# Modulation dot products moved from the branch tiles to the last values and the attention; the scale of two feature tiles by dot products on VectorE

## Chip, cores and metric

One core of one Trainium2 chip. The metric is the time of one execution on the device in microseconds. The kernel before takes 1518.03 us, the median of 3 runs (1517.66 to 1518.57).

## The reference

One layer of a diffusion transformer over 256 latent and 256 context tokens, model width 2048, all in float32. The conditioning vectors `c` and `c_ctx` give six modulation vectors by one large product; the latent tokens go through a mixer of two attentions with gates, then through a convolutional feed-forward part:

```python
mod = silu(c) @ w_mod + b_mod;  mod_c = silu(c_ctx) @ w_mod + b_mod
sh1, sc1, gt1, sh2, sc2, gt2 = split(mod, 6)
h  = modulate(rms_norm(x,   g_attn_pre), sh1,  sc1)      # y * (1 + scale) + shift
hc = modulate(rms_norm(ctx, g_attn_pre), csh1, csc1)
qa, ka, va, qb, kb, vb, ga, gb = split(h @ w_in);  ka_c, va_c, kb_c, vb_c from hc @ w_in
oa = window attention (8 heads, 2 key heads, rotary, sinks);  ob = neighbourhood attention (8 heads)
y  = (sigmoid(ga) * (oa @ w_br_a) + sigmoid(gb) * (ob @ w_br_b)) @ w_o
x  = x + gt1 * rms_norm(y, g_attn_post)
x  = x + gt2 * rms_norm(conv_ffn(modulate(rms_norm(x, g_ffn_pre), sh2, sc2)), g_ffn_post)
```

## The kernel before

Every float32 product is done as three matmuls: each operand is split into a high part (ScalarE, a copy with rounding, L127) and a low part (VectorE, source minus high, L131), and TensorE adds high·high, high·low and low·high. Weights come as blocks of 1 MB through the SP queue into a ring of four buffers `raw` and are split into `wh` and `wl`, in halves (`halves`, L136). `block(ahead)` gives the next block, splits the one after it and issues loads further ahead. The order on each engine is fixed when the kernel is built: by hand for TensorE in the two key sweeps, elsewhere by a scheduler that keeps what the tiles need of each other; `issue_after(x)` puts an instruction behind x.

The stages, by the trace: a first key sweep to about 97 us, a second key sweep to 153, the values to 263, the attention with the queries and three gates (`fill`) to 428, the gate stage (gates `pg` and branches `pb`) to 682, the output projection to 769, the up projection to 1268, the down projection to 1508.

**First key sweep.** Six key heads (NK1) over 16 feature tiles k, three matmuls `pk` per head and tile (`keys`). The modulation scale of tile k+1 comes from narrow matmuls `pm` (`narrow`, L313: the silu vectors as 32 columns against a 1 MB unit of `wm_sc`), is evacuated by ScalarE (`evacuated`), transposed by small matmuls `ptm` and becomes `Gc` on VectorE (`scale_of`, L334), and from this the scaled features `h` (L352 high, L354 low). From k=3 on two tiles are done at a time. The key weights of tile k are split into `ku`. Squares of the features go into `ssq` (`squares`); a matmul `pss` with ones (L514), in k=13 after the fourth head, sums them over partitions, and `rs` is the reciprocal root. The shift of four feature tiles (ND) comes from dot products on VectorE: `load_sd(t)` loads 1 MB of rows into the one buffer `sd`, and `dot` (L427) multiplies it with the silu vector of the latents (v=0) or of the context (v=1); `load_sd(t+1)` follows the second. The first two of these dots stand in k=12 and k=14, six in the second sweep.

**Modulation dots.** `mods` (L204) multiplies a 1 MB unit of `wm_b` from the ring with the broadcast silu vector `crb` on VectorE, one unit per dot; one unit is held ahead (`load_mod`). There are 48 of them up to the output projection. In the values, `beside(1)` puts 20 key bias dots and then mods next to the steps kk of each weight block; the last values block (nb == 9) has none. The attention has none. In the gate stage each gate has one, except gates (1,1) and (2,0), and branch tiles j = 4, 6, 8, 9, 10, 11, 13 have one, so that such a tile has three.

**Attention.** Period p does `scores` of head p on TensorE (`s`), a half `fill`, `transposes` of the head before (`pt`, split into `h`), the other half `fill`, and `values` of the head before (`po`, L792). In between, VectorE does the softmax, the split of the next weights, of the next keys (`keys_of`) and of the values (`vals_of`, the last two set `last`).

The lines that hold the places of the dots:

```python
if nb and kk < (0 if nb == 9 else 2 if nb == 8 else 3 if nb % 2 else 4):
    beside(1)
...
mods(1 if (j, i) not in ((1, 1), (2, 0)) else 0, crb[:])          # in gate(j, i)
...
mods(1 if j in (4, 6, 8, 9, 10, 11, 13) else 0, crb[:])           # in branch tile j
```

Of the kernel before, what the change touches and what calls it, by code (L numbers as in the profile page):

```python
# [58 lines left out]
def layer_kernel(ctx, tc, xc, xt, ccol, crow, wm_sc, wm_sd, wm_sh, wm_b, cols, wk, wkt, ws, rope, mask_a, bias_b, out):  # L59
# [181 lines left out]
    with ExitStack() as mx:  # L241
# [10 lines left out]
        with ExitStack() as at:  # L252
# [4 lines left out]
            def rope_of(t, which, nm):  # L257
# [58 lines left out]
            def evacuated(k, n, pm):  # L318
                ev = up.tile([P, 2 * P], F32, tag="half", bufs=2, name=f"ev{k}")
                with ExitStack() as es:  # L320
                    if k == KT - 2:
                        es.enter_context(tc.issue_after(done_u[k][0]))
                    e_ = nc.scalar.activation(ev[:, : n * P], pm[:, : n * P], AF.Copy)
# [126 lines left out]
            for k in range(KT):  # L450
# [861 lines left out]
```

## Time and profile before

| what | value |
|---|---|
| median of 3 runs | 1518.03 us |
| the profiled execution | 1517.4 us |
| its span from first to last instruction | 1515.6 us |
| mean granted clock of TensorE | 0.998 of full speed |
| TensorE busy | 1501.2 us, 99% |
| VectorE busy | 1132.8 us, 75% |
| ScalarE busy | 780.6 us, 52% |
| moved by DMA | 382.13 MB, 252 GB/s in the mean |

A row of the timeline reads: start, duration, engine, line, operation, output tile <- input tiles, shapes, count; in brackets the idle time of the engine before it and what released it. Durations of neighbouring rows overlap by some hundredths to 0.16 us, because instructions are pipelined; the distance of two starts is what one costs. A row of windows reads: stretch, its length, busy time of each engine with its instructions, granted clock, share of the DMA engines' time, GB/s. A row of groups reads: line, engine, operation, tiles, shapes, count, busy us and mean ns of one, then the idle time before.

### The profile page before, as it was taken

How to read it: one execution, taken by the hardware profiler on the slowest of the kernel's cores; microseconds unless marked ns; L12 is line 12 of the kernel's file. 1: busy time of each engine (PE TensorE's matmuls, PEld its weight loads, DVE VectorE, ACT ScalarE, POOL GpSimd, SP SyncE). 2: the span in 40 equal slices, each digit the busy share in tenths (PEclk: the TensorE clock that was granted, in tenths of full speed). 3: DMA queues.
4: the chain of work that ended last, by engine and by line, in shares of the span. 5: the costliest groups of instructions: out<-in, count | busy, mean ns of one | idle time of the engine just before them, and what ended most of it. 6: DMA issues, size and time to landing. Idle time of an engine off the chain costs nothing.

```text
span 1515.6 us, 21653 instructions
## 1 busy us (share of the span) xinstructions
PE 1501.2 (99%) x8549; PEld 1288.8 (85%) x8549; DVE 1132.8 (75%) x1679; ACT 780.6 (52%) x1277; POOL 1.7 (0%) x10
## 2 busy tenths in 40 slices
PE   9999999999999999999999999999999999999997
PEld 7876889899888888888888888888888888888886
DVE  4496996888888989887778888888788776444444
ACT  4442443777765544454466555555555555344342
POOL 0000000000000000000000000000000000000000
PEclk9999999999999999999999999999999999999999
DMA  9988678433378989888956666666666556555552
GB/s 369 398 321 336 270 295 331 160 133 112 122 258 299 348 327 344 330 332 345 378 192 223 250 232 220 244 248 227 245 240 234 195 193 251 221 194 195 194 194 84
DMA packets 59255, 382.13 MB, mean 252 GB/s; under 512 B 6545, under 2 KB 6929, under 8 KB 16913
## 3 DMA queue, kind: packets, MB, share of 16 engines
q1 hardware_dynamic: 58432, 379.68, 67.1%
q8 instruction: 67, 1.10, 0.3%
q10 hardware_dynamic: 720, 1.07, 0.2%
q14 instruction: 36, 0.29, 0.0%
HBM read 376.48 MB, written 4.24 MB: 251 GB/s over the span
## 4 chain that ended last, share of the span: by engine, by line
PE 95%; DVE 3%; ACT 1%; issue 0%; DMA 0%; DVEq 0%; SPq 0%
PE pu L174 21%; PE py_d L880 16%; PE pu L175 11%; PE pk L439 7%; PE pv L654 7%; PE pg L174 6%; PE py_o L880 5%; PE pq L174 4%; PE pb L174 3%; PE pg L175 3%; PE pq L175 2%; PE pb L175 2%; PE po L792 1%; PE s L762 1%; PE pm L313 1%; DVE wl L131 1%
## 5 line engine op out<-in xcount | busy, mean ns | idle before, releaser
L131 DVE TENSOR_TENSOR wl<-raw,wh 128x1024 fp32r<-128x1024 f32 x444 | 528.6, 1221 | 224.7 <-ACT wh L127 224.3
L127 ACT ACTIVATE wh<-raw 128x1024 fp32r<-128x1024 f32 x444 | 451.3, 1053 | 276.4 <-PE py_d L880 129.1
L174 PE MATMUL pu<-h,wh 128*128 128x512 f32 x1404 | 488.0, 391 | 0.0
L175 PE MATMUL pu<-h,wl 128*128 128x256 f32 x1404 | 395.9, 282 | 0.0
L174 PEld LDWEIGHTS pu<-h,wh 128*128 128x128 f32 x1404 | 263.6, 188 | 55.6 <-issue 0.4
L175 PEld LDWEIGHTS pu<-h,wl 128*128 128x128 f32 x1404 | 265.4, 189 | 0.0
L880 PE MATMUL py_d<-wh,ff 128*128 128x512 f32 x704 | 216.6, 389 | 0.0
L174 PE MATMUL pg<-h,wh 128*128 128x512 f32 x464 | 161.8, 390 | 0.0
L880 PEld LDWEIGHTS py_d<-wh,ff 128*128 128x128 f32 x704 | 132.1, 188 | 27.3
L204 DVE SCALAR_TENSOR_TENSOR raw<-raw,crb 128x2048 f32<-128x2048 f32 x64 | 146.2, 2286 | 7.3 <-DMA raw<-in_wm_b_dram 5.4
L880 PE MATMUL py_d<-wl,ff 128*128 128x512 f32 x352 | 136.9, 389 | 0.0
L175 PE MATMUL pg<-h,wl 128*128 128x256 f32 x464 | 131.4, 283 | 1.5 <-DVE wl L131 1.5
L439 PE MATMUL pk<-h,ku 128*128 128x512 f32 x480 | 118.0, 398 | 0.7 <-DVE ku L131 0.4
L179 ACT ACTIVATE half_u<-pu 128x256 f32<-128x256 f32 x88 | 33.5, 383 | 152.3 <-PE pu L175 152.3
L439 PEld LDWEIGHTS pk<-h,ku 128*128 128x128 f32 x480 | 87.4, 188 | 25.3 <-issue 4.8
L174 PE MATMUL pq<-h,wh 128*128 128x512 f32 x304 | 108.5, 395 | 0.0
L174 PEld LDWEIGHTS pg<-h,wh 128*128 128x128 f32 x464 | 87.1, 188 | 18.0
L654 PE MATMUL pv<-wh,h 128*128 128x512 f32 (+1 forms) x384 | 101.7, 354 | 0.0
L174 PE MATMUL pb<-h,wh 128*128 128x512 f32 x256 | 90.2, 392 | 0.9 <-ACT wh L127 0.9
L175 PEld LDWEIGHTS pg<-h,wl 128*128 128x128 f32 x464 | 87.7, 189 | 3.0 <-DVE wl L131 2.9
L175 PE MATMUL pq<-h,wl 128*128 128x256 f32 x304 | 85.5, 281 | 0.0
L180 DVE TENSOR_TENSOR u<-pu,half_u 128x256 f32<-128x256 f32 x88 | 37.2, 423 | 56.7 <-ACT half_u L179 56.6
(193 smaller groups left out, 1787.1 us busy)
## 6 DMA issues: line engine op xcount, KB each, us to landing
raw<-in_ws_dram SPq DMA_DIRECT2D x222, 1024.0 KB, 4.8
raw<-in_wm_b_dram SPq DMA_DIRECT2D x64, 1024.0 KB, 4.9
raw<-in_wm_sc_dram SPq DMA_DIRECT2D x15, 1024.0 KB, 7.7
raw<-in_wm_sh_dram SPq DMA_DIRECT2D x16, 768.0 KB, 6.3
raw<-in_wkt_dram SPq DMA_DIRECT2D x10, 1024.0 KB, 5.0
crb<-sild SPq DMA_DIRECT2D x6, 1024.0 KB, 7.2
raw<-in_wk_dram SPq DMA_DIRECT2D x7, 768.0 KB, 8.2
sd<-in_wm_sd_dram SPq DMA_DIRECT2D x4, 1024.0 KB, 7.5
```

The lines of the kernel that those rows point to most:

```text
L127: a_ = nc.scalar.activation(hi, src, AF.Copy)
L131: v_ = nc.vector.tensor_tensor(out=lo, in0=src, in1=hi, op=ALU.subtract)
L174: nc.tensor.matmul(pt[:, :], wh[:, w], a, start=first and i == 0, stop=False, skip_group_check=True)
L175: nc.tensor.matmul(pt[:, :S], wl[:, w], a[:, 0], start=False, stop=last and i == n - 1, skip_group_check=True)
L179: a_ = nc.scalar.activation(t[:], pt[:, S:], AF.Copy)
L180: v_ = nc.vector.tensor_tensor(out=out_, in0=pt[:, :S], in1=t[:], op=ALU.add)
L204: nc.vector.scalar_tensor_tensor(out=r, in0=r, scalar=1.0, in1=row, op0=ALU.mult, op1=ALU.mult, accum_out=modx[:, j : j + 1])
L313: nc.tensor.matmul(pm[32 * j : 32 * j + 32, t * P : t * P + P], cc[:, q, :], rsc[k + t][:, q * P : q * P + P], start=q < 4, stop=q >= KT - ...
L439: nc.tensor.matmul(pk[:], wt[:, w], hh[:, :, k, a], start=k == 0 and a == 0 and wt is wh, stop=k == KT - 1 and a == 1)
L654: nc.tensor.matmul(pv[i][:, :nw], src[:, k, a, t0 : t0 + P], wt[:, w], start=k == 0 and q == 0, stop=k == KT - 1 and q == 2)
L762: nc.tensor.matmul(s_ps[:], qs[hd][:, a, qt * P : qt * P + P], k_, start=q == 0, stop=q == 2)
L880: p_ = nc.tensor.matmul(py[t][:], act[:, k, a, t * P : t * P + P], wt[:, w], start=k == 0 and q == 0, stop=k == nk - 1 and q == 2)
```

## The change

It does three things.

1. The scale of the feature tiles 14 and 15 (NC = 2) is no longer done by narrow matmuls. Their rows of the modulation weights go ahead of the ND tiles in `wm_sd`, so that there are six tiles t for `dot`; t = 0 and 1 give the scales. `load_sd(0)` is issued in k=9 instead of k=10; dots stand in k=10 and k=11 (one each), k=12 (two), k=14 (one) and seven instead of six in the second sweep. `scale_of(14, 2)` reads the sums from `sd0`, in k=13 at the second head.
2. Seven mods of the branch tiles are moved: three to the last values block, four to the attention periods 1, 4, 7 and 10 (behind `last[1]`), and the gates (1,1) and (2,0) get the two that the numbering then leaves.
3. To hold one row of silu values `crb` from the values to the gates, tiles are placed otherwise: the rotary tables in two tiles, the masks in five rows of `bz` instead of seven (loaded alternately), and the second load of `crb` falls away.

```diff
+NC = 2
...
-            sh0 = sp.tile([P, ND, 2], F32, name="sh0")
+            sd0 = sp.tile([P, NC + ND, 2], F32, name="sd0")
...
             def load_sc(k):
-                if k < KT:
+                if k < KT - NC:
                     rsc[k] = raw_block(wm_sc[k], parts=1 if k else 2)
...
-            def scale_of(k, n, ev):
-
-                pt = bank(f"ptm{k}")
-                for t in range(n):
-                    nc.tensor.matmul(pt[:, 2 * t : 2 * t + 2], ev[:, t * P : t * P + P], sel[:], start=True, stop=True)
+            def scale_of(k, n, ev=None):
+
+                if ev is None:
+                    pt = sd0[:].rearrange("p a b -> p (a b)")
+                else:
+                    pt = bank(f"ptm{k}")
+                    for t in range(n):
+                        nc.tensor.matmul(pt[:, 2 * t : 2 * t + 2], ev[:, t * P : t * P + P], sel[:], start=True, stop=True)
...
             def load_sd(t):
-                if t < ND:
+                if t < NC + ND:
...
-                if k == 10:
+                if k == 9:
                     load_sd(0)
...
+                if k in (10, 11):
+                    dot(done_u[k + 1][1])
                 if k == 12:
 
+                    dot(done_u[k + 1][1])
                     d_ = dot(done_u[k + 1][1])
                     after = squares(14, done_u[k + 1][0], d_)
...
-                    n = 1 if k < 3 else 2 if k % 2 and k + 1 < KT else 0
+                    n = 1 if k < 3 else 2 if k % 2 and k + 1 < KT - NC else 0
...
+                    if k == KT - NC - 1 and i == 1:
+                        done = scale_of(k + 1, NC)
...
-                if k in (2, 3, 6, 7, 10, 11):
+                if k in (0, 2, 3, 6, 7, 10, 11):
                     dot(e_.ins)
...
-                            crb[0] = silu_row(cbp, "row", 2)
+                            crb[0] = silu_row(rowp, "row")
...
-                        if nb and kk < (0 if nb == 9 else 2 if nb == 8 else 3 if nb % 2 else 4):
+                        if nb and kk < (2 if nb == 8 else 3 if nb % 2 else 4):
                             beside(1)
...
-            bz = bzp.tile([P, 7, S], F32, name="bz")
-            sync.dma_start(out=bz[:, 2:4], in_=bias_b[0])
+            bz = bzp.tile([P, 5, S], F32, name="bz")
+            sync.dma_start(out=bz[:, 0:2], in_=bias_b[0])
...
+                if p in (1, 4, 7, 10):
+                    with tc.issue_after(last[1]):
+                        mods(1, crb[0][:])
...
-        crb = silu_row(gp)
+        crb = crb[0]
...
-            mods(1 if (j, i) not in ((1, 1), (2, 0)) else 0, crb[:])
+            mods(1, crb[:])
...
-            mods(1 if j in (4, 6, 8, 9, 10, 11, 13) else 0, crb[:])
...
-    o["wm_sd"] = w_mod[:, : ND * P].T.reshape(ND, P, D)
+    o["wm_sd"] = np.concatenate([w_mod[:, 2 * D - NC * P : 2 * D], w_mod[:, : ND * P]], axis=1).T.reshape(NC + ND, P, D)
-    o["wm_sc"] = units(w_mod[:, 2048:4096]).reshape(KT, P, D)
+    o["wm_sc"] = units(w_mod[:, D : 2 * D - NC * P]).reshape(KT - NC, P, D)
```

How the order moves, at three places.

**VectorE at the end of the first key sweep**, from the split of the key weights of tile 12 on. L131 or L132 is a split (`ku`), L427 a dot (its first operand is the tile of sums, `sh_112` or `sd_112`), L354 an `h`, L378 and L379 the squares. Before:

```order
L131 TENSOR_TENSOR ku_765<-raw_740,ku_765 128x768
L354 SCALAR_TENSOR_TENSOR h<-xn,Gc,h 128x256 x3
L378 TENSOR_TENSOR sq_826<-sq_826 128x512
L379 TENSOR_TENSOR ssq<-ssq,sq_826 128x512
L131 TENSOR_TENSOR ku_846<-raw_740,ku_846 128x768
L427 SCALAR_TENSOR_TENSOR kT,sh_112<-sd_742,crb_0_535 128x2048
L378 TENSOR_TENSOR sq_850<-sq_850 128x512
L379 TENSOR_TENSOR ssq<-ssq,sq_850 128x512
L131 TENSOR_TENSOR ku_874<-raw_842,ku_874 128x768
L334 TENSOR_SCALAR Gc<-ptm_918,col,bgc 128x2 x2
L354 SCALAR_TENSOR_TENSOR h<-xn,Gc,h 128x256 x4
L186 RECIPROCAL rs<-rs 128x512
```

The same stretch with the change (the dot of t0 with the latents, t0v0, stands three rows further up):

```order
L132 TENSOR_TENSOR ku_766<-raw_742,ku_766 128x768
L427 SCALAR_TENSOR_TENSOR sd_661,sd_112<-sd_661,crb_0_638 128x2048
L354 SCALAR_TENSOR_TENSOR h<-xn,Gc,h 128x256 x3
L378 TENSOR_TENSOR sq_826<-sq_826 128x512
L132 TENSOR_TENSOR ku_846<-raw_742,ku_846 128x768
L379 TENSOR_TENSOR ssq<-ssq,sq_826 128x512
L334 TENSOR_SCALAR Gc<-sd_112,col,bgc 128x2
L354 SCALAR_TENSOR_TENSOR h<-xn,Gc,h 128x256 x2
L427 SCALAR_TENSOR_TENSOR kT,sd_112<-sd_770,crb_0_535 128x2048
L427 SCALAR_TENSOR_TENSOR sd_770,sd_112<-sd_770,crb_0_638 128x2048
L378 TENSOR_TENSOR sq_853<-sq_853 128x512
L132 TENSOR_TENSOR ku_877<-raw_842,ku_877 128x768
```

The dot t0v1 now stands ahead of the three `h` of tiles 12 and 13, and the two dots of t1 (`sd_770`) stand ahead of the last squares, whose sum `ssq` follows as the next row and is what `pss` reads. On SP, `sd_661` (t0) is issued ahead of `wm_sc` 12 and 13; `sd_770` waits for t0v1, and the key weights of tiles 14 and 15 stand behind it.

**VectorE in the attention, from period 1 to period 2** (L766 or L776 is the softmax's first step on the scores, L708 or L719 the query, `wl` the next weights' split). Before:

```order
L131 TENSOR_TENSOR h<-vv,h 128x512
L131 TENSOR_TENSOR wl_2568<-raw_2472,wh_2567 128x1024
L708 SCALAR_TENSOR_TENSOR rq_2523<-pq_2474,qb_2524 128x256
L766 ISA sm_0_2551,st_2546<-s_0_2547,bz 128x512
L766 ISA st_2546 128x1
L766 ISA sm_1_2561,st_2546<-s_1_2557,bz 128x512
```

With the change:

```order
L132 TENSOR_TENSOR h<-vv,h 128x512
L205 SCALAR_TENSOR_TENSOR raw_2161,modx<-raw_2161,crb_0_1921 128x2048
L719 SCALAR_TENSOR_TENSOR rq_2503<-pq_2454,qb_2504 128x256
L776 ISA sm_0_2534,st_2529<-s_0_2530,bz 128x512
L776 ISA st_2529 128x1
L132 TENSOR_TENSOR h<-rq_2503,h 128x256
L780 TENSOR_SCALAR st_2529<-st_2529 128x1
L776 ISA sm_1_2544,st_2529<-s_1_2540,bz 128x512
```

A mod (L205) stands behind the split of the values, and the next weights' split has moved behind the softmax's first step. On TensorE the value matmuls `po` of such a period, twelve in a row before, now are one, then two score matmuls of the next head, then eleven. The five mods lie in periods 1, 4, 7, 10 and 11; the last of them is the one of gate (1,1), for which the scheduler found this earlier place.

**VectorE in the gate stage, one tile with a mod of its branch** (L180 or L181 adds halves of `pg` or `pb`, L860 or L872 is gate times branch). Before:

```order
L204 SCALAR_TENSOR_TENSOR raw_5594,modx<-raw_5594,crb_6_4084 128x2048
L180 TENSOR_TENSOR g_0_5597<-pg_0_5561,half_g_0_5598 128x256
L180 TENSOR_TENSOR g_1_5646<-pg_1_5610,half_g_1_5647 128x256
L131 TENSOR_TENSOR wl_5652<-raw_5608,wh_5651 128x1024 x2
L204 SCALAR_TENSOR_TENSOR raw_5643,modx<-raw_5643,crb_6_4084 128x2048
L180 TENSOR_TENSOR bt_0_5684<-pb_0_5667,half_b_0_5685 128x256
L860 TENSOR_TENSOR g_0_5285<-g_0_5285,bt_0_5684 128x256
L131 TENSOR_TENSOR wl_5715<-raw_5657,wh_5714 128x1024
L180 TENSOR_TENSOR bt_1_5706<-pb_1_5689,half_b_1_5707 128x256
L131 TENSOR_TENSOR wl_5715<-raw_5657,wh_5714 128x1024
L860 TENSOR_TENSOR g_1_5334<-g_1_5334,bt_1_5706 128x256
L204 SCALAR_TENSOR_TENSOR raw_5659,modx<-raw_5659,crb_6_4084 128x2048
```

The same tile with the change:

```order
L181 TENSOR_TENSOR g_0_5584<-pg_0_5548,half_g_0_5585 128x256
L205 SCALAR_TENSOR_TENSOR raw_5630,modx<-raw_5630,crb_0_1921 128x2048
L132 TENSOR_TENSOR wl_5639<-raw_5595,wh_5638 128x1024
L181 TENSOR_TENSOR g_1_5633<-pg_1_5597,half_g_1_5634 128x256
L132 TENSOR_TENSOR wl_5639<-raw_5595,wh_5638 128x1024
L181 TENSOR_TENSOR bt_0_5668<-pb_0_5651,half_b_0_5669 128x256
L872 TENSOR_TENSOR g_0_5275<-g_0_5275,bt_0_5668 128x256
L132 TENSOR_TENSOR wl_5699<-raw_5644,wh_5698 128x1024
L181 TENSOR_TENSOR bt_1_5690<-pb_1_5673,half_b_1_5691 128x256
L132 TENSOR_TENSOR wl_5699<-raw_5644,wh_5698 128x1024
L872 TENSOR_TENSOR g_1_5324<-g_1_5324,bt_1_5690 128x256
L205 SCALAR_TENSOR_TENSOR raw_5739,modx<-raw_5739,crb_0_1921 128x2048
```

Three mods before, two now; the splits and sums are the same.

## Rows read from the trace of the kernel before

**Rows 1.** The page: busy time of each engine, and the slices of VectorE.

```profile
PE 1501.2 (99%) x8549; PEld 1288.8 (85%) x8549; DVE 1132.8 (75%) x1679; ACT 780.6 (52%) x1277; POOL 1.7 (0%) x10
DVE  4496996888888989887778888888788776444444
```

**Rows 2.** The gate stage. From TensorE's timeline the first branch matmul of four tiles; from the list of TensorE's waits in 600 to 682 us (us in total, times, longest) its two rows; from VectorE's groups in 628.4 to 661.7 us the mods; from the windows the first tile.

```profile
444.50 0.39 PE L174 MATMUL pb<-h,wh 128*128 128x512 f32 x1
...
461.14 0.39 PE L174 MATMUL pb<-h,wh 128*128 128x512 f32 x1
...
611.01 0.39 PE L174 MATMUL pb<-h,wh 128*128 128x512 f32 x1
...
665.60 0.39 PE L174 MATMUL pb<-h,wh 128*128 128x512 f32 x1
...
PE pg L175 <- DVE wl L131: 1.5, 2, 0.7
PE pb L174 <- ACT wh L127: 0.9, 2, 0.5
...
L204 DVE SCALAR_TENSOR_TENSOR raw<-raw,crb 128x2048 f32<-128x2048 f32 x5 | 11.4, 2284 | 0.0
...
444.50:461.10 16.60, 16.60 (x98) 14.71 (x97) 14.33 (x18) 8.36 (x13) 0.00 (x0) 1.00 0.81 306
```

**Rows 3.** TensorE's timeline, 70 to 97 us: the blocks of narrow matmuls, the keys between them, `pss`.

```profile
70.89 1.95 PE L313 MATMUL pm<-raw,cc 128*32 128x128 f32 x64
...
73.94 7.79 PE L439 MATMUL pk<-h,ku 128*128 128x512 f32 x33
81.66 1.95 PE L313 MATMUL pm<-raw,cc 128*32 128x128 f32 x64
83.54 0.96 PE L439 MATMUL pk<-h,ku 128*128 128x512 f32 x3
84.34 0.50 PE L332 MATMUL ptm<-sel,ev 128*128 128x2 f32 x4
84.70 1.63 PE L439 MATMUL pk<-h,ku 128*128 128x512 f32 x6
86.17 1.02 PE L514 MATMUL pss<-ssq,kT 128*128 128x512 f32 x2
```

**Rows 4.** The first sweep's transfers: the window of 62 to 74 us, SP's issues of the scales of tiles 12 and 13, and from the list of DMA issues (count, KB each, us from issue to landing) the one of tile 13 (issued in 61 to 61.6 us) and the `sd` issued in 94 to 95 us.

```profile
62.00:74.00 12.00, 12.00 (x116) 9.85 (x112) 5.35 (x10) 4.91 (x9) 0.00 (x0) 1.00 1.02 416
...
58.64 2.95 SPq L120 DMA_DIRECT2D raw<-in_wm_sc_dram  x2
...
raw<-in_wm_sc_dram SPq DMA_DIRECT2D x1, 1024.0 KB, 8.9
...
sd<-in_wm_sd_dram SPq DMA_DIRECT2D x1, 1024.0 KB, 5.3
```

**Rows 5.** VectorE's timeline, 74 to 91 us.

```profile
74.11 0.47 DVE L334 TENSOR_SCALAR Gc<-ptm,col,bgc 128x2 f32<-128x2 f32 x2 [4.74 <-PE ptm L332]
...
75.71 0.96 DVE L131 TENSOR_TENSOR ku<-raw,ku 128x768 fp32r<-128x768 f32 x1 [0.25 <-ACT ku L127]
76.59 1.27 DVE L354 SCALAR_TENSOR_TENSOR h<-xn,Gc,h 128x256 fp32r<-128x256 f32 x3
...
80.06 2.28 DVE L427 SCALAR_TENSOR_TENSOR kT<-sd,crb 128x2048 f32<-128x2048 f32 x1
...
82.28 0.68 DVE L378 TENSOR_TENSOR sq<-sq 128x512 f32<-128x512 f32 x1
82.99 0.69 DVE L379 TENSOR_TENSOR ssq<-ssq,sq 128x512 f32<-128x512 f32 x1
83.60 0.95 DVE L131 TENSOR_TENSOR ku<-raw,ku 128x768 fp32r<-128x768 f32 x1
...
85.74 1.68 DVE L354 SCALAR_TENSOR_TENSOR h<-xn,Gc,h 128x256 fp32r<-128x256 f32 x4 [0.39 <-ACT h L352]
```

**Rows 6.** TensorE's clock: its last matmul, the two windows behind it (the clock is the column before the DMA share), and from TensorE's groups the keep-busy matmuls in 0 to 5.2 us and in 5.2 to 10 us.

```profile
1507.45 0.39 PE L880 MATMUL py_d<-wl,ff 128*128 128x512 f32 x1
...
1507.90:1510.40 2.50, 0.00 (x0) 0.00 (x0) 1.77 (x4) 0.95 (x3) 0.00 (x0) 1.00 0.15 57
1510.50:1515.60 5.10, 0.00 (x0) 0.00 (x0) 1.63 (x3) 0.00 (x0) 0.00 (x0) 0.50 0.54 207
...
L236 PE MATMUL busy<-ident 128*128 128x128 f32 x14 | 3.4, 432 | 1.9 <-POOL ident masks.py:199 1.9
...
L236 PE MATMUL busy<-ident 128*128 128x128 f32 x9 | 1.8, 311 | 0.0
```

**Rows 7.** The attention: VectorE's split of the second head's keys and TensorE's first scores of that head; an early and a late period by windows; VectorE's last splits in that late one, period 12, and TensorE's value matmuls.

```profile
280.08 0.67 DVE L131 TENSOR_TENSOR h<-kT,h 128x512 fp32r<-128x512 f32 x1
...
281.20 0.62 PE L762 MATMUL s<-h 128*128 128x512 f32 x2
...
299.65:308.87 9.22, 9.22 (x60) 8.30 (x59) 7.69 (x19) 6.51 (x15) 0.00 (x0) 1.00 0.42 144
381.30:390.50 9.20, 9.20 (x60) 8.13 (x59) 9.19 (x25) 7.19 (x16) 0.00 (x0) 1.00 0.33 118
...
389.54 1.28 DVE L131 TENSOR_TENSOR h<-pt,h 128x512 fp32r<-128x512 f32 x2
...
391.18 1.45 PE L792 MATMUL po<-h 128*128 128x256 f32 x11
```

More of the change, by code (lines that the diff above doesn't have):

```diff
@@ L261, in rope_of @@
                     nc.scalar.activation(tr[a : a + 64, :], t[b : b + 64, :], AF.Copy)
-                nc.vector.tensor_tensor(out=t, in0=t, in1=rp[:, 2 * which], op=ALU.mult)
-                nc.vector.tensor_tensor(out=tr[:], in0=tr[:], in1=rp[:, 2 * which + 1], op=ALU.mult)
+                nc.vector.tensor_tensor(out=t, in0=t, in1=rp[which][:, 0], op=ALU.mult)
+                nc.vector.tensor_tensor(out=tr[:], in0=tr[:], in1=rp[which][:, 1], op=ALU.mult)
                 nc.vector.tensor_tensor(out=t, in0=t, in1=tr[:], op=ALU.add)
             kv = at.enter_context(ExitStack())
-            hcp = kv.enter_context(tc.tile_pool(name="hcp", bufs=1))
+            st = kv.enter_context(ExitStack())
+            hcp = st.enter_context(tc.tile_pool(name="hcp", bufs=1))
             shc = hcp.tile([P, 2, KT], F32, name="shc")
-            st = kv.enter_context(ExitStack())
             sp = st.enter_context(tc.tile_pool(name="sp", bufs=1, side="right"))
@@ L319, in evacuated @@
                 ev = up.tile([P, 2 * P], F32, tag="half", bufs=2, name=f"ev{k}")
[L320 to L323, printed above, removed]
+                e_ = nc.scalar.activation(ev[:, : n * P], pm[:, : n * P], AF.Copy)
                 if k < 5:
@@ L428, in dot @@
                         out=rsd[t][:] if v else junk, in0=rsd[t][:], scalar=1.0, in1=shrow[v], op0=ALU.mult, op1=ALU.mult,
-                        accum_out=sh0[:, t, v : v + 1]).ins
+                        accum_out=sd0[:, t, v : v + 1]).ins
                 if v:
-                    nc.vector.tensor_scalar(
-                        out=shc[:, :, t], in0=sh0[:, t], scalar1=col[:, C_BMOD + t : C_BMOD + t + 1], scalar2=None, op0=ALU.add)
+                    if t >= NC:
+                        f = t - NC
+                        nc.vector.tensor_scalar(
+                            out=shc[:, :, f], in0=sd0[:, t], scalar1=col[:, C_BMOD + f : C_BMOD + f + 1], scalar2=None,
+                            op0=ALU.add)
                     load_sd(t + 1)
@@ L509, in layer_kernel @@
                             units[k + 1] = unit(k + 1)
-                        if k not in (1, KT - 3):
+                        if k != 1:
                             after = squares(k // 2 * 2 if n == 1 else k + 1, done[0])
@@ L598, in layer_kernel @@
             vv = vp.tile([P, 4, 1280], F32, name="vv")
+            rowp = mx.enter_context(tc.tile_pool(name="rowp", bufs=1))
             cbp = kv.enter_context(tc.tile_pool(name="cbp", bufs=1))
-            rp = vp.tile([P, 4, S], F32, name="rp")
-            sync.dma_start(out=rp, in_=rope)
+            rp = [(vp, cbp)[i].tile([P, 2, S], F32, name=f"rp{i}") for i in range(2)]
+            for i in (1, 0):
+                sync.dma_start(out=rp[i], in_=rope[:, 2 * i : 2 * i + 2])
             shr = []
             for v in range(2):
-                shr.append(cbp.tile([P, D], F32, tag="row", bufs=2, name=f"shr{v}"))
+                shr.append((cbp, rowp)[v].tile([P, D], F32, tag="row", name=f"shr{v}"))
                 sync.dma_start(out=shr[v], in_=shd[v].partition_broadcast(P))
@@ L751, in scores @@
                 kh, kl = keys_of(hd)
-                b0 = 0 if is_a else 2 + 2 * (hd % 2)
+                b0 = 0 if is_a else 2 * (hd % 2)
                 n = hd + 1 - NHA
-                if 0 < n < NHB:
-                    sync.dma_start(out=bz[:, 2 + 2 * (n % 2) : 4 + 2 * (n % 2)], in_=bias_b[n])
-                elif n == NHB:
-                    sync.dma_start(out=bz[:, 0:2], in_=mask_a)
+                if 0 < n <= NHB:
+                    sync.dma_start(out=bz[:, 2 * (n % 2) : 2 + 2 * (n % 2)], in_=bias_b[n] if n < NHB else mask_a)
                 st_ = at2.tile([P, 2, 4], F32, tag="st", bufs=3, name=f"st{hd}")
@@ L767, in scores @@
                         out=sm[:].rearrange("p (a b) -> p a b", a=2), in0=s_ps[:].rearrange("p (a b) -> p a b", a=2),
-                        in1=bz[:, b0 + qt : 7 : 6 - b0 - qt], op0=ALU.add, op1=ALU.max, scale=1.0,
+                        in1=bz[:, b0 + qt : 5 : 4 - b0 - qt], op0=ALU.add, op1=ALU.max, scale=1.0,
                         scalar=col[:, C_SINK + hd : C_SINK + hd + 1] if is_a else -3.0e38, accum_out=m)
```

2 lines of the change are left out of this document (1 added, 1 removed).

## The prediction

> **What bounds the kernel now.** I read the page's totals first, then the waits of TensorE, then the two stretches that the change touches. TensorE is busy for 1501.2 of 1515.6 us and VectorE for 1132.8 [rows 1], so a change can gain only where it takes work off TensorE or ends a wait of TensorE, and it loses wherever VectorE, now given more beside the sweeps, makes TensorE wait. The slices of VectorE [rows 1] are an average that hides this: its digits go from 4 to 9 and the moved work goes into places that have to be read one by one.
>
> The clearest waits are in the gate stage. One tile j of it takes 16.64 us between the first branch matmuls (444.50 to 461.14) where nothing is late; from 611.01 to 665.60, three tiles, it takes 54.59 us [rows 2]. Three times 16.64 is 49.92, so 4.67 us are lost there. The waits of that stretch name the lower and the upper half of a weight split. A tile with two modulation dots keeps VectorE busy for 14.33 of 16.60 us; such a dot takes 2.28 us, so a tile with a third one has 16.6 of 16.64: VectorE is full there, any moment in which it waits for ScalarE's half of a split is not made good, and the tile is late [rows 2].
>
> **The change part by part.** The profiled execution took 1517.4 us (span 1515.6); the median of the runs is 1518.03. The sum is made against the first and carried to the second.
>
> 1. *Narrow matmuls removed.* TensorE's timeline has the block of tiles 14 and 15 at 81.66: 64 narrow matmuls until 83.54 (1.88 us), and the four small ones from 84.34 to 84.70 (0.36) [rows 3]. They stand on the path: **−2.2 us**.
>
> 2. *sd0 issued early.* The first megabyte of dot weights now goes ahead of the scales of tiles 12 and 13 in SP's queue. That stretch moves 416 KB per us with the DMA engines at 1.02 of their time [rows 4], so one megabyte costs 2.5 us. Tile 13's scale is issued at 61.26 (58.64 + 2.95 − 0.33) and lands 8.9 us later, at 70.2; it would land at 72.7. Its narrow matmuls are the second half of the block at 70.89, from about 71.83 [rows 3]. So 0.9 us of wait, less if the queue takes it in another order: **+0.8** (0 to 0.9).
>
> 3. *Dot t0v1 ahead of three h's.* Before, VectorE went from the split at 75.71 straight to three h's at 76.59 [rows 5], and the third matmul of tile 12 needs the first of these, at about 77.1 (the 33 matmuls from 73.94 take 7.72 us until 81.66, so 0.234 us each; twelve belong to tile 11, tile 12 starts at 76.75). A dot takes 2.28 us, with 2.2 to the next instruction (80.06 to 82.28) [rows 5]. The order puts one between, so the h comes 2.2 us later: **+2.1**.
>
> 4. *pss behind two more dots.* The sum of squares over the partitions (pss, 86.17 [rows 3]) is in TensorE's order after the fourth head of tile 13. Its input was complete at 83.68 [rows 5], 2.5 us early. Now VectorE must first do both dots of t1, a key split and the h's of tile 14. Adding up the rows from the split of tile 12's half, shifted by 0.8 to 76.5: split 0.9, dot 2.25, three h's 1.3, sq 0.7, split 0.85, ssq 0.65, Gc 0.25, two h's with their wait for ScalarE 1.4, two dots 4.4, sq 0.7, split 0.85, ssq 0.65: 91.4 to 91.7 [rows 5]. The landing of sd1 costs this chain 0.2 us at most: it is issued when t0v1 is done, at 79.7, into a queue that has run empty, and a lone one landed in 5.3 us [rows 4], at 85.0, while VectorE comes to it at 84.8; behind it on SP wait the key weights of tiles 14 and 15, some 2 us later, and their split is due at 89. TensorE arrives at 86.7 (80.1 + 16 and 12 matmuls of 0.234) and waits 5.0 us: **+5.0** (4.0 to 6.0). Together steps 1 to 4 move pss from 86.17 to 91.8, +5.7. Later tiles and the second sweep, with one dot more, keep the order and the distances they had.
>
> 5. *The clock.* [...] What it costs is bounded from below by 0 (it does not fall) and from above by the start: the first 14 matmuls, 0.24 us apart for 3.35 us, mean 432 ns each against 311 for the same instruction later [rows 6], which I read as the lower level. Half of 3.3 us: **+1.6** (0 to 3.2, twice as long).
> [...]
>
> 6. *Attention.* Three dots go into the last values block, five are now done within the attention (four by their rule, one that the scheduler pulls in). Values: TensorE is held by nothing there and the weights land early. At the entry, the lower half of the second head's keys ends at 280.75; the third score matmul after 281.20 needs it, at 281.7 [rows 7]; in the new order it stands behind both scalings and the second half of a split, a little over 1 us later: **+0.3** (0 to 1). In the periods of 9.2 us VectorE is busy 7.69 early and 9.19 in a late one [rows 7]. A dot of 2.28 overruns an early period by 0.75, which the next period takes back, and the order now has two score matmuls go ahead of most of the value matmuls, which covers it. Late, two dots fall into periods 10 and 11, right ahead of the full one: its last two splits end at 390.82, and the value matmuls that need them stand at 391.18 [rows 7], 0.4 away; a lag of some 1.3 leaves about 1.0. With some tenths at each of the others, **+1.5** for all (0 to 4: five overruns of 0.75 and nothing covered).
>
> 7. *Gates.* The branch tiles lose 7 dots; two are left per tile, the load of the stretch from 444.50 to 461.10 in which TensorE is busy throughout [rows 2]. All of the loss goes: **−4.6** (−4.67 to 0). The two gates at the entry get a dot each, which gives their tile the load of the one just named: 0.
>
> 8. *The rest.* One row load less (1 MB before the gates, when the DMA queue is not full), smaller tiles for masks and tables, masks loaded in turn: 0, covered by loads that are issued a period ahead; uncovered, one landing of some 5 us. The wait added at the row load of the silu values stands a transfer later and behind it weights that have a block in hand.
>
> Sum: −2.2 + 0.8 + 2.1 + 5.0 + 1.6 + 0.3 + 1.5 − 4.6 = **+4.5**: 1521.9 for a profiled execution, 1522.5 against the median of 1518.03.
>
> **The rivals.**
> [...]
> - *The first sweep hides the dots* (not slower). Place: pss. If VectorE reaches the complete ssq by 86.7, terms 2 to 5 vanish and the removal stands: −2.2 + 0.3 + 1.5 − 4.6 = −5.0, 1513.0. It decides at whether the two dots of t1 stand ahead of ssq: each one that runs after it gives back 2.2. For it: VectorE idles 4.74 us just before 74.11 [rows 5]. Against: the order of the instructions is fixed, and only one dot lies in that gap.
> - *VectorE binds the attention.* The overruns are not covered (4.0 instead of 1.5, entry 1.0 instead of 0.3): +7.7, 1525.7. For it: 9.19 of 9.20 in the late period. Against: the early periods have 1.5 us free, and four of the five dots are not followed by a full one.
> - *The gates do not get faster* (the change doesn't do there what it could): the splits wait for transfers and not for VectorE; term 7 is 0, +9.1, 1527.1. Against: the waits name splits, and tiles with two dots have none.
>
> **How the numbers follow.** Chances: forecast 0.42, clock holds 0.22, dots hidden 0.14, attention bound 0.10, gates unchanged 0.06, something else 0.06. No change, as a measurement here can tell it, is within 0.2%, 3.0 us: 1515.0 to 1521.1. The forecast's own bounds (pss ±1, attention 0 to 4) leave 0.10 of its 0.42 within it; the clock rival lies on the edge, 0.12 within; something else counts 0.05 within and 0.01 faster. Faster 0.15, same 0.27, slower 0.58. The range leaves out the hidden dots below and the unchanged gates above (0.20): from the clock rival with its other terms at their lower bounds (1520.9 − 1.8 − 0.8 − 1.0 = 1517.3) down to 1517.0, to the bound attention with a part of the longer low clock, 1527.0.
>
> **What would show it.** Right: pss at 91 to 92 us, with VectorE's dots of t1 right before its ssq; a wait of TensorE of 2 us within tile 12; a granted clock of 0.5 for some us after pss; the branch matmuls 16.64 us apart in all tiles from 561 on, shifted; scores of the second head some tenths late, and a wait of about 1 us around period 12. Wrong: pss at 84 to 87, or tiles of the gate stage still at 18 us, or more than 4 us of waits in the attention.

## The result and the profile after

The changed kernel takes **1521.09 us** (median of 10 runs, 1519.62 to 1523.86) against 1517.64 us of the kernel before (10 runs, 1517.35 to 1518.57): ratio 1.0024, 95% interval 1.0015 to 1.0033. It is slower, by 3.5 us. The forecast was 1522.5; the profiled execution of the changed kernel took 1520.66 us (forecast 1521.9).

The page after has TensorE at 1500.2 us in 1518.8, 1.0 us less work than before, and VectorE at 1141.6 us, 8.8 us more [rows 1]:

```profile
PE 1500.2 (99%) x8481; PEld 1288.4 (85%) x8481; DVE 1141.6 (75%) x1687; ACT 780.8 (51%) x1276; POOL 1.6 (0%) x10
```

So there is less to do on TensorE and the kernel is longer: TensorE waits, or works at a lower clock. The places are found by comparing, in both traces, the start of the first matmul of each stage on TensorE (us from the span's start; `pmsh` are the narrow matmuls of the shift in the second sweep, `ptsh` its transposes near the end of that sweep):

| first matmul of | before | after | difference | added in the stretch before it |
|---|---|---|---|---|
| pss (squares summed over partitions) | 86.17 | 91.31 | +5.13 | +5.1: first sweep up to pss |
| pmsh (second sweep) | 100.08 | 108.00 | +7.92 | +2.8: rest of the first sweep |
| s (attention) | 274.27 | 282.16 | +7.89 | 0.0: second sweep and values |
| pg (gate stage) | 427.86 | 436.28 | +8.42 | +0.5: attention |
| py_o (output projection) | 682.24 | 685.99 | +3.75 | −4.7: gate stage |
| last instruction ends | 1515.61 | 1518.78 | +3.17 | −0.6: the rest, untouched by the change |

Of the +5.1 of the first row, 0.3 us is there already at 24 us (a block of narrow matmuls starts at 23.65, in the kernel before at 23.34), ahead of everything that the change moves. In the mods alone, an experiment below, the same block starts at 23.72, 0.4 us late.

**First sweep.** TensorE's timeline, 71 to 98 us, answers to [rows 3]:

```profile
71.23 2.22 PE L313 MATMUL pm<-raw,cc 128*32 128x128 f32 x64
73.38 0.98 PE L442 MATMUL pk<-h,ku 128*128 128x512 f32 x3
74.19 0.50 PE L332 MATMUL ptm<-sel,ev 128*128 128x2 f32 x4
74.55 3.48 PE L442 MATMUL pk<-h,ku 128*128 128x512 f32 x14
79.95 6.65 PE L442 MATMUL pk<-h,ku 128*128 128x512 f32 x28 [1.92 <-DVE h L354]
91.31 2.04 PE L522 MATMUL pss<-ssq,kT 128*128 128x512 f32 x2 [4.71 <-DVE ssq L379]
92.36 5.96 PE L442 MATMUL pk<-h,ku 128*128 128x512 f32 x14
```

The second narrow block is gone, and two waits stand in brackets that the kernel before did not have: 1.92 us inside tile 12 for an h, and 4.71 us at pss for the squares. The last row is the third sign: 14 matmuls in 5.96 us, 0.43 us each, where [rows 3] have 0.234. VectorE's timeline from 74.7 us on shows who is late; it answers to [rows 5]:

```profile
76.33 0.96 DVE L132 TENSOR_TENSOR ku<-raw,ku 128x768 fp32r<-128x768 f32 x1 [0.25 <-ACT ku L128]
77.20 2.29 DVE L427 SCALAR_TENSOR_TENSOR sd<-sd,crb 128x2048 f32<-128x2048 f32 x1
...
79.42 1.27 DVE L354 SCALAR_TENSOR_TENSOR h<-xn,Gc,h 128x256 fp32r<-128x256 f32 x3
...
84.45 2.29 DVE L427 SCALAR_TENSOR_TENSOR kT<-sd,crb 128x2048 f32<-128x2048 f32 x1
...
86.78 2.29 DVE L427 SCALAR_TENSOR_TENSOR sd<-sd,crb 128x2048 f32<-128x2048 f32 x1
...
89.00 0.69 DVE L378 TENSOR_TENSOR sq<-sq 128x512 f32<-128x512 f32 x1
89.61 0.95 DVE L132 TENSOR_TENSOR ku<-raw,ku 128x768 fp32r<-128x768 f32 x1
90.47 0.68 DVE L379 TENSOR_TENSOR ssq<-ssq,sq 128x512 f32<-128x512 f32 x1
```

A row "..." stands for rows left out: accumulator reads of 0.08 us and, between 80.61 and 84.45, squares, a key split, a scale and two h's. At 77.20 the dot t0v1 runs while TensorE stands for the h of 79.42; at 84.45 and 86.78 the two dots of t1 run while the sum that pss needs is complete only at 91.15. From 77.20 to 91.15 VectorE idles once, for 0.58 us, behind ScalarE: its order is the wait. The clock in windows (granted clock third from the end):

```profile
86.00:91.30 5.30, 0.60 (x3) 0.20 (x2) 5.26 (x8) 0.84 (x1) 0.00 (x0) 0.90 0.86 317
91.30:97.00 5.70, 5.70 (x12) 3.78 (x13) 3.84 (x4) 2.44 (x4) 0.00 (x0) 0.50 0.98 359
97.00:102.00 5.00, 5.00 (x23) 4.14 (x22) 3.70 (x5) 1.06 (x1) 0.00 (x0) 1.00 0.89 327
```

TensorE's granted clock went from 1.00 to 0.50 about 1 us before the wait ended (0.90 over 5.30 us) and came back at about 97.0. In the 5.70 us of the middle row it did 12 matmuls, half of the 24 that 0.234 us each would give, which is the 2.8 us of the table.

**Gates.** First branch matmuls of the same four tiles, a window of the first tile, and the mods of the two tiles from 636.07 to 669.35 us, against [rows 2]:

```profile
452.92 0.39 PE L175 MATMUL pb<-h,wh 128*128 128x512 f32 x1
...
469.56 0.39 PE L175 MATMUL pb<-h,wh 128*128 128x512 f32 x1
...
619.43 0.39 PE L175 MATMUL pb<-h,wh 128*128 128x512 f32 x1
...
669.35 0.39 PE L175 MATMUL pb<-h,wh 128*128 128x512 f32 x1
...
452.92:469.52 16.60, 16.60 (x98) 14.71 (x97) 14.19 (x18) 8.37 (x13) 0.00 (x0) 1.00 0.75 278
...
L205 DVE SCALAR_TENSOR_TENSOR raw<-raw,crb 128x2048 f32<-128x2048 f32 x4 | 9.1, 2284 | 0.0
```

Three tiles take 49.92 us (669.35 − 619.43), exactly 3 × 16.64, where they took 54.59. TensorE's list of waits has no row in the gate stage any more. One thing in the kernel before is easily missed: the tile from 511.06 us also has three mods, VectorE is busy for 16.54 of its 16.64 us, and it is not late; two more with three mods, from 577.62, take 16.67 and 16.72 us, as the same tiles do with the change. The whole loss lies in the three tiles from 611.01 us, which take 17.13, 18.81 and 18.65 us, where tiles with a third mod follow each other (8 to 11 of the code). So one full tile is not late by itself, and no run tells how few of the seven mods had to move.

In the attention the list has one row, 0.2 us:

```profile
PE s L772 <- ACT h L128: 0.2, 1, 0.2
```

### The profile page after: what moved, and what is told of

Read it like the earlier page. It is cut to its first block, busy times and chain, and to the rows that moved or that the text cites. A ratio compares the mean times of both kernels' runs of the same rounds, so it can differ in the third digit from the quotient of the medians.

```text
span 1518.8 us, 21515 instructions
## 1 busy us (share of the span) xinstructions
PE 1500.2 (99%) x8481; PEld 1288.4 (85%) x8481; DVE 1141.6 (75%) x1687; ACT 780.8 (51%) x1276; POOL 1.6 (0%) x10
## 4 chain that ended last, share of the span: by engine, by line
PE 95%; DMA 2%; DVE 1%; ACT 1%; issue 0%; DVEq 0%; SPq 0%; ACTq 0%
PE pu L175 21%; PE py_d L892 16%; PE pu L176 11%; PE pv L665 7%; PE pg L175 7%; PE py_o L892 6%; PE pk L442 6%; PE pq L175 4%; PE pb L175 4%; PE pg L176 4%; PE pq L176 2%; PE pb L176 2%; PE s L772 1%; PE po L802 1%; DMA raw<-in_wm_sc_dram 1%; PE pt L793 1%
## 5 line engine op out<-in xcount | busy, mean ns | idle before, releaser
L132 DVE TENSOR_TENSOR wl<-raw,wh 128x1024 fp32r<-128x1024 f32 x444 | 529.9, 1221 | 220.9 <-ACT wh L128 220.6
L205 DVE SCALAR_TENSOR_TENSOR raw<-raw,crb 128x2048 f32<-128x2048 f32 x64 | 146.2, 2285 | 10.2 <-DMA raw<-in_wm_b_dram 9.7
L180 ACT ACTIVATE half_u<-pu 128x256 f32<-128x256 f32 x88 | 33.5, 383 | 152.6 <-PE pu L176 152.6
L181 DVE TENSOR_TENSOR u<-pu,half_u 128x256 f32<-128x256 f32 x88 | 37.1, 423 | 56.7 <-ACT half_u L180 56.6
```

The costliest lines, as they stand in the source:

```text
L132: v_ = nc.vector.tensor_tensor(out=lo, in0=src, in1=hi, op=ALU.subtract)
L180: a_ = nc.scalar.activation(t[:], pt[:, S:], AF.Copy)
L181: v_ = nc.vector.tensor_tensor(out=out_, in0=pt[:, :S], in1=t[:], op=ALU.add)
L205: nc.vector.scalar_tensor_tensor(out=r, in0=r, scalar=1.0, in1=row, op0=ALU.mult, op1=ALU.mult, accum_out=modx[:, j : j + 1])
```

## The experiments

My theory after the result: the whole loss comes from the dots of the scale in the first sweep (VectorE's order, and then the clock); the mods' move is a clean gain. The rival: the parts act together, for instance the moved mods or the tiles placed otherwise cost time in the sweeps.

**The mods alone.** The kernel before with points 2 and 3 of the change; the scales stay with the narrow matmuls.

```diff
+                if p in (1, 4, 7, 10):
+                    with tc.issue_after(last[1]):
+                        mods(1, crb[0][:])
...
-            mods(1 if j in (4, 6, 8, 9, 10, 11, 13) else 0, crb[:])
```

> Only the moved modulation dots; the first key sweep as before. Theory (the loss sits in the sweep alone, the gates give 4.67 us): gates at 16.64 us per tile, attention about 0.5 us longer, no wait at pss, no fall of the clock: 1517.6 - 4.7 + 0.5 - 0.3 = about 1513.2. Rival (the dots cost the attention as much as they free): at or above 1516.5, with waits of over 2 us between the first scores and the gates.

Measured: **1513.10 us** (1512.79 to 1513.34), ratio 0.9969 (0.9958 to 0.9980), faster than both kernels. pss starts at 86.58 (+0.41, there already at 24 us, and no wait near it), pg +0.93, py_o −3.74: 0.5 us lost in the attention, 4.7 won in the gates. From pss to pmsh it takes 13.91 us, as before:

```profile
86.58 1.02 PE L513 MATMUL pss<-ssq,kT 128*128 128x512 f32 x2
87.03 13.53 PE L438 MATMUL pk<-h,ku 128*128 128x512 f32 x57
100.49 0.85 PE L542 MATMUL pmsh<-raw,cc 128*32 128x384 f32 x8
```

That is the table's lower half without its upper half.

**The scales alone.** The kernel before with point 1 only.

```diff
-                    n = 1 if k < 3 else 2 if k % 2 and k + 1 < KT else 0
+                    n = 1 if k < 3 else 2 if k % 2 and k + 1 < KT - NC else 0
...
+                if k in (10, 11):
+                    dot(done_u[k + 1][1])
```

> Only the scales of tiles 14 and 15 by dots; modulation dots as before. Theory: pss 5 us later, clock at half for 5 to 7 us, gate stage again 4.67 us long: 1517.6 + 5.1 + 2.8 = about 1525.5, with a spread of the runs of some us as in the change. Rival (the loss came from the new placement of tiles and loads): 1520 or less.

Measured: 1525.37 us (1524.72 to 1526.04), ratio 1.0052 (1.0039 to 1.0064). pmsh +7.80, then flat to the end, with the gate stage's old waits in place. The two parts add up: −4.5 + 7.8 = +3.3, and together they gave +3.5. The rival falls. TensorE's waits in 60 to 100 us, the matmuls behind the wait in tile 12, then the windows:

```profile
PE pss L523 <- DVE ssq L380: 3.1, 1, 3.1
PE pk L443 <- DVE h L355: 1.9, 1, 1.9
PE pm L314 <- DMA raw<-in_wm_sc_dram: 1.2, 1, 1.2
...
80.92 8.25 PE L443 MATMUL pk<-h,ku 128*128 128x512 f32 x28 [1.93 <-DVE h L355]
...
79.00:82.40 3.40, 1.48 (x6) 1.24 (x7) 3.40 (x7) 3.38 (x4) 0.00 (x0) 1.00 0.27 51
82.40:85.80 3.40, 3.40 (x9) 2.63 (x8) 2.82 (x6) 1.11 (x4) 0.00 (x0) 0.50 0.94 387
85.80:92.60 6.80, 3.72 (x16) 2.74 (x15) 6.47 (x8) 1.11 (x2) 0.00 (x0) 1.00 0.90 329
92.60:96.05 3.45, 3.45 (x8) 2.21 (x7) 2.25 (x3) 1.34 (x3) 0.00 (x0) 0.51 1.01 389
```

Here the clock fell twice, and the first time 1.5 us after the wait of 1.9 us had ended (80.92), while matmuls already ran. The row of DMA is term 2: here tile 13's scale landed 1.2 us late. The runs do not spread as expected: they lie 1.3 us apart, not some us as those of the changed kernel do.

**Filling the wait at pss.** The changed kernel with 18 small matmuls of a constant ahead of pss, whose result nothing uses.

```diff
                     if k == KT - 3 and i == 3:
+                        keep_busy(18, "w")
                         pss = bank("pss")
```

> The change with 18 keep-busy matmuls (128x128) in TensorE's order ahead of pss, whose result nobody reads. Theory (the clock falls because TensorE idles 4.7 us): the clock stays at 1.0, 2.8 us less than the change, about 1518.2, and the runs lie closer together than the 4.2 us of the change. Rival (the fall has another cause, or the keep-busy matmuls themselves delay pss): 1520.5 or more, clock still 0.5 after pss or pss later than 92.

Measured: 1520.92 us (1518.97 to 1522.31), ratio 1.0021 (1.0013 to 1.0030): no better, a miss. The clock stayed up behind pss and fell elsewhere, behind the wait in tile 12:

```profile
80.03 8.26 PE L442 MATMUL pk<-h,ku 128*128 128x512 f32 x28 [1.91 <-DVE h L354]
88.13 4.18 PE L237 MATMUL busy_w<-ident 128*128 128x128 f32 x36
92.15 1.02 PE L523 MATMUL pss<-ssq,kT 128*128 128x512 f32 x2
...
81.50:85.00 3.50, 3.50 (x10) 2.69 (x9) 2.92 (x6) 1.12 (x4) 0.00 (x0) 0.51 0.95 391
85.00:93.00 8.00, 8.00 (x54) 6.97 (x52) 7.18 (x10) 1.75 (x3) 0.00 (x0) 1.00 0.91 342
```

The 28 matmuls at 80.03 take 8.26 us where the changed kernel needs 6.65. So the filler starts some 1.5 us later than it would have at the full clock, and ends at 92.15, 1.0 us after the sum was complete (91.14): it delays pss by 0.8 us against the changed kernel, which the expectation had named as a rival. Behind pss the gain is there: 13.89 us to pmsh, where the changed kernel takes 16.69, so that pmsh stands at 106.04, 2.0 us earlier. Of this, 1.3 us is lost again in the second sweep (15.14 us between its third and fourth blocks of `pmsh`, from 133.68, where the changed kernel takes 13.82). A wait of 0.36 us for a key split, which the changed kernel does not have, is part of it; the rest is not explained. The profiled execution is 0.8 us faster than that of the changed kernel, the median 0.2.

**A better order of VectorE.** Both tiles still by dots, but t0's two dots run together in the idle stretch at 69 to 74 us, the last squares stand ahead of t1's dots, the reciprocal root stands behind the last h, and the dot that was last in the first sweep goes into the second. Part of the edit:

```diff
-                if k in (10, 11):
+                if k == 10:
+                    dot(done_u[k + 1][1])
                     dot(done_u[k + 1][1])
...
-                        done = scale_of(k + 1, NC)
+                        done = scale_of(k + 1, 1)
+                        dot(done[1])
+                        dot(done[1])
+                        done = scale_of(k + 2, 1)
...
-                if k in (0, 2, 3, 6, 7, 10, 11):
+                if k in (0, 1, 2, 3, 6, 7, 10, 11):
```

> The change with its dots in other places of VectorE's order: both of t0 ahead of the scale of tile 12, the squares and ssq ahead of both dots of t1, the reciprocal behind the last h, the dots of t2 behind the evacuation of the keys (eight in the second sweep). Theory (the order, not the work, made pss wait): no wait of TensorE over 1 us in the sweep, pss at 84 to 85, clock 1.0; about 1511.5 to 1513, below the moved dots alone by 0 to 2 us. Rival (VectorE has not the time, or sd1 lands too late): waits move to tile 14 or 15 or to the evacuation, 1515 or more.

Measured: 1517.44 us (1515.96 to 1517.83), ratio 0.9996 (0.9987 to 1.0004), the rival. pss came at 84.21, 2.0 us earlier than in the kernel before, with no wait: the order was the cause of the 4.7 us. But by the second sweep's first matmul nothing was left of it (pmsh +0.01): the reciprocal (3.35 us on VectorE) now stands behind t1's dots, and the first keys of the second sweep wait 1.1 us until the first sweep's keys are evacuated behind it (`kT`). ptsh stood at +3.3. TensorE's waits in 60 to 156 us:

```profile
PE pk L445 <- DVE ku L132: 3.1, 3, 2.1
PE pk L445 <- DVE kT L531: 1.1, 1, 1.1
PE pk L445 <- ACT h L355: 0.2, 1, 0.2
```

VectorE had 27.50 of 27.50 us busy from 96.50 to 124.00. The dots had only been pushed on to where it is full, and the order, which decided at pss, is not enough for the whole.

**Only t0v1 moved.** The changed kernel with t0's two dots at k = 10, and (in a part of the edit not shown) the scales of tiles 14 and 15 behind those of 12 and 13.

```diff
-                if k in (10, 11):
+                if k == 10:
+                    dot(done_u[k + 1][1])
                     dot(done_u[k + 1][1])
```

> The changed kernel, but the second dot of t0 runs right behind the first, in the idle stretch of VectorE at 69 to 74 us, and no longer ahead of the three h of tile 12 (the scale of tile 14 from it stays behind the scales of tiles 12 and 13). Theory (VectorE's chain sets pss): the wait of 1.9 us in tile 12 goes, the chain to ssq is 2.2 us shorter, pss at 89.1 us (91.3 before this edit). TensorE arrives at 84.7 and waits 4.4 us, the granted clock still falls there; 1518.9 us against 1521.1 of the changed kernel. Rival (the landing of the second megabyte sets the chain): pss stays at 91.3, 1521. Rival (a single wait of 4.4 us costs no clock): pmsh at 103.0, 1516.1.

Measured: 1516.66 us (1514.84 to 1519.61), ratio 0.9993 (0.9984 to 1.0003). pss at 89.22: the chain of VectorE is 2.1 us shorter, as expected, and the wait in tile 12 is gone. But the clock did not fall in the profiled execution, although TensorE stood for 3.2 us (4.4 expected; a wait of 1.28 us for tile 13's scale took the rest). The time is nearer to the rival without a cost of the clock (1516.1) than to the theory (1518.9):

```profile
89.22 1.10 PE L526 MATMUL pss<-ssq,kT 128*128 128x512 f32 x2 [3.21 <-DVE ssq L382]
...
86.00:89.20 3.20, 0.01 (x1) 0.01 (x1) 3.20 (x6) 0.68 (x2) 0.00 (x0) 1.00 1.03 416
89.20:96.00 6.80, 6.78 (x28) 5.30 (x29) 6.38 (x7) 1.87 (x4) 0.00 (x0) 1.00 0.68 233
```

From pss to pmsh it took 13.99 us, as before (13.91) and with the filler (13.89); in the changed kernel 16.69. That is the price of the low clock by itself, 2.7 to 2.8 us.

**The same with the wait filled.** As the last one, with the 18 small matmuls ahead of pss.

```diff
                     if k == KT - 3 and i == 3:
+                        keep_busy(18, "w")
                         pss = bank("pss")
```

> The kernel with the early second dot of t0, and 18 small matmuls of a constant tile (4.2 us in an earlier run) ahead of pss, which fill the wait there and compute nothing that is used. Now no wait above 0.6 us is left ahead of pss. Theory (the low clock behind a wait of TensorE costs about 2.8 us): pss stays at 89.1, the granted clock stays at 1.0 through the first key sweep, pmsh comes 2.8 us earlier than without the 18 matmuls, 1516.1. Rival (the clock is a by-product, VectorE's chain on to the evacuation of the key heads sets the second sweep's start): pmsh and the time as without them, 1518.9.

Measured: 1517.06 us (1516.34 to 1518.66), ratio 0.9994 (0.9985 to 1.0003), between the theory and the rival. pss 89.24 and pmsh 103.12, as without the filler (89.22 and 103.21): in the two profiled executions the clock held in both, so there was nothing to win, and the median did not improve. What the clock does over the runs is told by the mean granted clock that each run lists:

| kernel | runs at 0.999 | at 0.998 | at 0.997 or lower |
|---|---|---|---|
| changed kernel | none | none | 1519.62 to 1523.86 (10) |
| better order | 1515.96 to 1516.33 (3) | 1516.26 to 1517.83 (5) | 1517.59 to 1517.77 (3) |
| only t0v1 moved | 1514.84 to 1515.83 (3) | 1515.96 to 1518.05 (6) | 1517.81, 1519.61 |
| the same, filled | 1516.34 to 1518.66 (7) | 1516.52 to 1517.39 (4) | none |

In the two middle kernels of the table, whose waits stay open, the runs at 0.997 are 1.3 us or more longer than those at 0.999, and with the wait filled no run is below 0.998. That the clock makes this part of the spread is read from the table, not from traces of those runs, and other kernels bear it out less well: in the changed kernel with pss's wait filled the one run at 0.997 (1521.19) is as long as one at 0.999 (1521.17), and of the dots alone the one run at 0.998 (1525.37) lies amid those at 0.996. What share of the spread the clock has is not shown.

**One tile instead of two.** NC = 1: only tile 15 by dots, both in the idle stretch; everything after stands as in the kernel before.

```diff
-NC = 2
+NC = 1
...
-                    n = 1 if k < 3 else 2 if k % 2 and k + 1 < KT - NC else 0
+                    n = 1 if k < 3 or k == KT - 3 else 2 if k % 2 and k + 1 < KT - NC else 0
```

> As the changed kernel, but only feature tile 15 gets its scale from dots (NC = 1): its two dots stand in VectorE's idle stretch at 69 to 74 us, tile 14 keeps its 32 narrow matmuls, all later dots stand where they stand in the kernel before, and the mods are moved. Theory (a removed block of TensorE pays where VectorE has room for the dots in that place): half of the 2.2 us of narrow matmuls goes at no cost, -1.1 against the kernel with the moved mods alone (1513.1): 1512.0. Rival (the load of the dot weights ahead of the scales, or the later h, costs more than the 1.1): 1513.1 to 1515.

Measured: 1515.43 us (1513.64 to 1517.30), ratio 0.9983 (0.9974 to 0.9992): slower than the mods alone, the rival, a little beyond its end. The 1.1 us are removed, and in the profiled execution (1515.54) more is given back, 2.5 us of it in three places that the trace names:

```profile
73.00 1.08 PE L313 MATMUL pm<-raw,cc 128*32 128x128 f32 x32 [0.93 <-DMA raw<-in_wm_sc_dram]
...
93.48 7.85 PE L448 MATMUL pk<-h,ku 128*128 128x512 f32 x32 [0.45 <-DVE ku L132]
...
PE pv L671 <- DVE wl L132: 1.1, 1, 1.1
```

The dot weights ahead of the scales in SP's queue make tile 13's scale 0.93 us late; the h of tile 15 stands where it holds VectorE 0.83 us and with it a key split; and the values wait 1.1 us for a weight split. Its runs lie 3.7 us apart at 0.998 and 0.999, without order between clock and time; what spreads them is not settled.

**The second sweep's dots later.** The better order, with the eight dots at k = 0, 3, 6, 7, 10, 11, 12, 13.

```diff
-                if k in (0, 1, 2, 3, 6, 7, 10, 11):
+                if k in (0, 3, 6, 7, 10, 11, 12, 13):
```

> The kernel with both tiles by dots in the better order of VectorE, in which pss came at 84.2 and the second sweep waited 3.1 us for key splits, with the eight dots of the second sweep spread later (k = 0, 3, 6, 7, 10, 11, 12, 13 in place of 0, 1, 2, 3, 6, 7, 10, 11). Theory (the second sweep lost only by the order, VectorE idles 5.4 us at its end): the waits of 3.1 us go, 1514.3. Rival (VectorE has no room in both sweeps together): the waits move to another place, 1516 to 1517.5.

Measured: 1516.31 us (1515.84 to 1518.03), ratio 0.9993 (0.9984 to 1.0002): the rival. The second sweep lost all but 0.4 of its 3.1 us of waits for key splits (ptsh +0.73, as pmsh), and the values' first split became late, behind the last two dots:

```profile
146.67 1.23 DVE L132 TENSOR_TENSOR ku<-ru,ku 128x1024 fp32r<-128x1024 f32 x1 [9.15 <-ACT ku L128]
147.81 2.29 DVE L430 SCALAR_TENSOR_TENSOR kT<-sd,crb 128x2048 f32<-128x2048 f32 x1
...
150.14 2.29 DVE L430 SCALAR_TENSOR_TENSOR sd<-sd,crb 128x2048 f32<-128x2048 f32 x1
...
152.35 1.22 DVE L132 TENSOR_TENSOR wl<-raw,wh 128x1024 fp32r<-128x1024 f32 x1
...
PE pv L669 <- DVE wl L132: 2.1, 1, 2.1
```

VectorE's 9.15 idle us before 146.67 stay unused: in its order the last two dots stand behind that key split, which waits for ScalarE. Whether an order exists in which all dots of both tiles fit is left open; none of the four that ran (the changed kernel's among them) is as fast as the mods alone.

## Why the prediction was right, and where its sizes were off

The mechanism and the sign were right, and the number was 1.4 us off. That it came so near is in part luck: the two terms that were mis-sized, +1.2 and −1.3 us, cancel. By its steps:

1. *Narrow matmuls removed* (−2.2): the block is gone from the trace. The better order shows what is left of it where nothing waits: pss 2.0 us earlier than before.
2. *sd0 issued early* (+0.8): 0.26 in the profiled run, where the block at 71.23 takes 2.15 us to the next matmul instead of 1.88. In the other profiled runs that load sd0 early it is 0.3 to 1.3 us, in four of the seven above the bound of 0.9 that I gave.
3. *t0v1 ahead of the h's* (+2.1): 1.92.
4. *pss behind t1's dots* (+5.0): 4.71; VectorE's sum was predicted at 91.4 to 91.7 and was complete at 91.15. With it, pss moved by 5.1 (5.7 predicted), 0.3 of which has nothing to do with these steps, as it is there at 24 us.
5. *The clock* (+1.6): the step that was mis-sized. It fell and cost 2.8. No run shows the +1.6: that a wait in the middle of the work brings the clock down as the end of the kernel did (from 1.00 to 0.50, 2.6 us after the last matmul [rows 6]), and for one stretch of the start's length, 3.3 us at half, was my estimate. What the changed kernel showed in its place is a clock at 0.50 from about 90.2 to 97.0, twice as long, and only its first 1 us lay in the wait. The predicted bound of 3.2 had foreseen this case. The start was a poor measure: its 14 matmuls run at 0.24 us each, where the same matmul in the filler takes 0.12 (36 in 4.18 us), but the granted clock of that stretch (1.95 to 5.30 us) stands at 1.00, so that no row ever showed it at 0.50. Steps 1 to 5 together were +7.3 and measured +7.9.
The traces give no length of wait from which the clock falls: a wait of 1.9 us was followed by a fall in two kernels (to 0.50 and 0.51) and by none in the changed one, one of 3.2 us by none, and at the end of the kernel before the fall came 2.6 us after the last matmul [rows 6]. Nor does it fall in idle time alone: in those two kernels it fell 1.5 us after the wait had ended, in the middle of matmuls.
6. *Attention* (+1.8 with its entry): 0.5, and the mods alone give the same 0.5. The second mis-sized term: I let each overrun of a period leave some tenths, and the list of waits has a single one of 0.2, at the scores of 380.46, where nearly all of the 0.5 arises. The entry cost nothing (the second head's scores stand at 289.09, +7.89 like the first's), and the wait of about 1 us around period 12 did not come. That the early score matmuls cover the other overruns is my reading of the order; no run tests it.
7. *Gates* (−4.6): −4.67 measured between pg and py_o, all of it; the late tiles are 16.64 us apart now. The reason I gave, that a tile with three mods is late because VectorE is full, is too simple: three tiles of that kind were in time in the kernel before, and the loss came only where they follow each other.
8. *The rest* (0): between py_o and the end the changed kernel is 0.6 us shorter, in code that no one changed. The mods alone gained as much there and the dots alone nothing. 0.2 of it is a shorter wait of the up projection (0.3 for 0.5 us), the rest comes after the last stores are issued; why is open.

Steps 1 to 4 came out 0.6 below the sum, 5 came out 1.2 above it, 6 1.3 and 7 0.1 below, 8 0.6 below: +4.5 − 1.3 is the +3.2 of the trace. Of the rivals, the one in which the clock stays at 1.00 through the wait at pss (1520.9) was nearer to the measured median than the forecast, and is refuted for the changed kernel by the window at 0.50, so that the time alone could not have told the two apart. In the profiled execution with one dot moved the clock did hold.

## What to carry to other kernels

An engine that is 75% busy on the page can still be full in the stretch where work is moved to it: 2.2 us of TensorE were removed at the price of four dots of 2.28 us on VectorE, in two sweeps in which none of the orders that ran found a place for them, while the seven dots that were moved out of a full stage into emptier ones brought 4.7 us for 0.5. Split such a change and time the halves: the half that pays (1513.10 us) was hidden behind the half that doesn't. And where the order on an engine is fixed, ask of every moved instruction which result stands behind it; a wait of a few us then costs its own length and can cost the lower clock after it, here 2.8 us.

## What the runs showed of the hardware

- TensorE's clock can fall in the middle of a busy kernel, and when it does is not told by the length of the wait: after 1.9 us of waiting in tile 12 it fell in two kernels (dots alone: 0.50 in 82.40 to 85.80 us; pss's wait filled: 0.51 in 81.50 to 85.00) and held in the changed kernel after the same wait (1.00 from 70.80 to 84.00); after 3.2 us at pss it held as well (only t0v1 moved: 1.00 from 86.00 on).
- The fall can begin when the wait is over: in two cases the low stretch lies wholly in matmuls that follow it, and 28 matmuls took 8.25 and 8.26 us instead of the changed kernel's 6.65.
- The runs of these kernels spread differently, and the clock alone does not explain it: the changed kernel's lie 4.2 us apart, those of the kernel before 1.2 and of the mods alone 0.6; but the dots alone, where the clock falls twice in the trace, lie only 1.3 us apart, and the kernel with one tile by dots, where it does not fall, 3.7.
